# Modulation rows stored from adjacent partitions, tokens scaled in place, eight modulation pieces moved behind the recurrence

## The chip, the cores and the metric

The kernel runs on one core of a Trainium2 chip (trn2). The metric is the device time of one execution in microseconds (us); single instructions are given in nanoseconds (ns) where that is plainer. The engines are PE (matrix products, results in PSUM banks), DVE (vector operations), ACT (activations and copies), POOL (general vector work) and SP (issues most DMAs, in order). All engines run on their own and wait for one another by semaphores.

## The reference

Two layers of a diffusion trunk over 512 latent and 256 context tokens of width 1024, in float32. What matters here is the head of each layer:

```python
mod = sc @ w_ada[l] + b_ada[l]        # sc = silu(c), 6 x 1024 columns
modc = scc @ w_ada[l] + b_ada[l]      # scc = silu(c_ctx)
sh1, s1, g1, sh2, s2, g2 = jnp.split(mod[:, None, :], 6, axis=-1)
h = rmsnorm(x, norm1_g[l]) * (1 + s1) + sh1
p = jnp.split(h @ w_in[l], split_at, axis=-1)
```

The parts of `p` feed four mixers: A, a gated linear recurrence (HGRN); B, a long convolution (Hyena) whose filters are computed from small networks and turned into spectra; C, neighbourhood attention; D, latent attention. Their outputs go through one output projection, and a mixture of experts follows. The normalisation is `x * rsqrt(mean(x^2) + eps)` per token, then gain, scale and shift per column.

## The kernel before, in words

**Memory.** One large tile, the `arena`, holds nearly all working tiles as column ranges; `Scope` and `E.t` hand out the ranges, first fit. A second tile, `side`, holds weights in flight. PSUM banks come from small pools: `pw` has two banks and serves the projections (L1283), the modulation pieces (L1177, L1187) and, in layer 0, the transposes of the tokens.

**Order of the work.** The program is written in the order of the model, and the framework's scheduler places each engine's instructions: what stands earlier in the program goes first when it is ready, and later work fills the gaps. So what is written behind a loop can run beside it.

**Modulation (class `Ada`).** `w_ada` of a layer is used in 24 pieces. A piece (`step`) loads two halves of 512 KB by SP (L1175) into a ring buffer `araw`, does 8 products of 128x32 by 128x256 on PE (L1177; the profile records 16), four groups of input rows side by side in 32 PSUM partitions each, and ACT copies the result (L1182) into `part[g]`. After every eighth piece the four groups are added (L1187, a 0/1 matrix `sum4`), the bias is loaded (L1190, 128x512) and added on DVE (L1192), and two DMAs (L1194) store the row to DRAM (`modd`); the row's eight used lines lie 32 partitions apart (`row[v:128:32]`). `cols` (L1204 to L1210) turns the first row into columns, the scale `mcs` and the shift `mcb`, by four 128x128 transposes.

**Where the pieces run.** Pieces 0 to 7 of layer 0 run first (`boot`, 16 buffers). While they run, the first constants and the six token tiles `x` are loaded (L1461), at piece 4. The others are called by `more`: after each projection, `STEPS[n]` of them, and behind the recurrence, `STEPH` of them, through a ring of three buffers. Before, `STEPS` is one piece after each of the first eight projections, none after two and one after each of the last six, with `STEPH = 10`: 24 in all (16 of layer 0, 8 of layer 1).

**Head of a layer.** `row_scales` squares the token rows (ACT L1227, DVE L1224, a scratch `hfull`), forms `rsqrt` on DVE (L1132 to L1145) and scales an identity by it (L1232) for each of six token tiles. `normed_T` multiplies each 128x128 block of `x` by that scaled identity (L1247), which transposes and normalises at once; ACT (L1250) and DVE (L1251) apply scale and shift, and the high and low parts `hh`, `hl` are formed (L1252). Four latent and two context tiles, eight column blocks each: 48 blocks for a layer.

**Projections and filters in layer 0.** `Proj.cols` loads 128 columns of `w_in` (L1274), splits them (ACT L1258, POOL L1259) and does 24 matmuls for the latent and 24 for the context tokens (L1283). The order is two columns each for i, q, g, then four for z, the recurrence (`hgrn`, L219 to L313, six levels of DVE work L241 to L268 and then a serial scan L291), then six u for the convolution. Between the projections the filters are computed by the generator `spectra`: for each of three filters it loads `w3`, `decay`, `tun`, `fwd`, `rot`, folds the filter (`filter_fold`, L409 to L445, ends in the sum L443) and stores its spectra (`filter_spectra`, L460 to L469, stores `spd`). `FOLD0` and `FOLDS` say how many steps of it go where; all of it stands ahead of z.

## Time and profile before

| | |
|---|---|
| median of 3 runs | 2461.41 us (2459.84 to 2464.67) |
| profiled execution, its time | 2464.16 us |
| its span | 2462.1 us |
| PE busy | 2059.6 us (84%) |
| DVE busy | 1055.0 us (43%) |
| ACT, POOL busy | 614.7 us (25%), 586.8 us (24%) |
| HBM | 240 GB/s over the span |

Busy times are means over the whole span, in which layers 0 and 1 each go through a front (projections, mixers) and an expert stage that streams weights. The span is the profiled part of one execution; the time of that execution is the one with which its durations belong. Each L number is a line of the kernel.

### The profile page before, as it was taken

Reading aid. Unit: us, or ns where it says so; the run is one execution under the profiler, and the core shown is the slowest. Engines: PE = TensorE matmul, PEld = TensorE weight load, DVE = VectorE, ACT = ScalarE, POOL = GpSimd, SP = SyncE. Lnnn points to the kernel's source line nnn. Section 1 sums busy time; section 2 is a strip of 40 time slices with the busy share of each in tenths; the row PEclk is TensorE's granted clock in tenths of the full one; section 3 lists DMA queues with packets and bytes.
Section 4 is the critical chain, followed back from the end, with each engine's and each line's share of the span. In section 5 each row is a group of like instructions: output and inputs, shape, how many; then the busy total and the mean of one; then the engine's idle time right before and its main releaser. Section 6 shows DMA issues by size and latency. Waiting matters only on the chain.

```text
span 2462.1 us, 32352 instructions
## 1 busy us (share of the span) xinstructions
PE 2059.6 (84%) x11460; PEld 1200.1 (49%) x11460; DVE 1055.0 (43%) x2495; ACT 614.7 (25%) x1205; POOL 586.8 (24%) x477
## 2 busy tenths in 40 slices
PE   5888889999999588887777598899899688877775
PEld 2555667866679433322222286676668433222221
DVE  5753885546865622222112437754584611111111
ACT  2445632143541100000000235324352110000000
POOL 1553732312003211211111236331101212111111
PEclk7999999999999699999999799999999699999998
DMA  7343424301242799999999624431233799999996
GB/s 274 129 152 126 164 88 152 100 26 52 84 139 78 275 379 371 405 401 403 401 403 397 226 86 154 134 124 35 73 116 118 283 390 409 411 407 409 411 404 255
DMA packets 139316, 581.57 MB, mean 236 GB/s; under 512 B 23984, under 2 KB 47873, under 8 KB 88630
## 3 DMA queue, kind: packets, MB, share of 16 engines
q1 hardware_dynamic: 124054, 555.89, 58.4%
q0 software_dynamic: 15008, 22.36, 3.8%
q8 instruction: 151, 2.47, 0.4%
q14 instruction: 103, 0.84, 0.1%
HBM read 554.17 MB, written 36.80 MB: 240 GB/s over the span
## 4 chain that ended last, share of the span: by engine, by line
PE 32%; DMA 25%; another core or an unknown queue 18%; DVE 12%; issue 4%; ACT 3%; POOL 2%; SPq 0%; ACTq 0%; POOLq 0%; DVEq 0%
PE pw L1283 11%; DMA acc<-arena 8%; DMA out_dram<-arena 7%; DMA arena<-h2d,arena 6%; PE pw L1804 4%; PE pb L609 2%; PE pa L789 1%; PE pb L529 1%; PE pb L511 1%; DMA spd<-arena 1%; DVE arena L265 1%; DVE arena L266 1%; PE pb L592 1%; PE pb L995 1%
## 5 line engine op out<-in xcount | busy, mean ns | idle before, releaser
L995 PE MATMUL pb<-side,arena 128*64 128x512 f32 x1224 | 288.0, 604 | 45.7 <-DMA side<-in_w_moe 42.1
L999 DVE COPY arena<-pb 128x512 f32<-128x512 f32 x67 | 46.3, 691 | 502.9 <-PE pb L995 502.9
L995 PE MATMUL pb<-arena 128*64 128x512 f32 x920 | 221.1, 616 | 38.3 <-DMA arena<-in_w_moe 34.8
L1011 ACT ACTIVATE arena<-pb 128x256 f32<-128x256 f32 x67 | 25.8, 384 | 901.7 <-PE pb L1008 901.7
L1259 POOL TENSOR_TENSOR wl<-side,wh 128x1024 fp32r<-128x1024 f32 x52 | 125.6, 2416 | 399.3 <-ACT wh L1258 200.8
L995 PEld LDWEIGHTS pb<-side,arena 128*64 128x64 f32 x1224 | 81.1, 137 | 246.5 <-issue 126.8
L1283 PE MATMUL pw<-hh,wh 128*128 128x512 f32 (+1 forms) x720 | 170.1, 369 | 5.8 <-ACT arena L1559 2.1
L1026 DVE SCALAR_TENSOR_TENSOR arena<-pb,arena 128x512 f32<-128x512 f32 x67 | 50.3, 751 | 261.5 <-PE pb L1022 253.5
L1283 PE MATMUL pw<-hh,wl 128*128 128x512 f32 (+1 forms) x720 | 161.0, 357 | 0.0
L1283 PE MATMUL pw<-hl,wh 128*128 128x512 f32 (+1 forms) x720 | 158.2, 354 | 0.0
L995 PEld LDWEIGHTS pb<-arena 128*64 128x64 f32 x920 | 63.3, 140 | 189.9 <-issue 101.6
L1022 PE MATMUL pb<-side,arena 128*64 128x512 f32 x576 | 135.4, 609 | 22.4 <-DVE arena L1012 21.9
L1035 POOL DMA_INDIRECT acc<-arena x35 | 55.2, 1578 | 388.4 <-DVE arena L1030 341.6
L1283 PEld LDWEIGHTS pw<-hh,wh 128*128 128x128 f32 x720 | 119.5, 192 | 41.0 <-issue 15.0
L1022 PE MATMUL pb<-arena 128*64 128x512 f32 x496 | 115.7, 607 | 21.8 <-DVE arena L1012 20.2
L1283 PEld LDWEIGHTS pw<-hl,wh 128*128 128x128 f32 x720 | 117.2, 189 | 24.0 <-issue 8.2
L1283 PEld LDWEIGHTS pw<-hh,wl 128*128 128x128 f32 x720 | 117.3, 190 | 23.0 <-issue 8.0
L1035 POOL DMA_INDIRECT out_dram<-arena x32 | 50.9, 1590 | 311.8 <-DVE arena L1026 297.3
L973 POOL DMA_INDIRECT arena<-h2d,arena x67 | 69.8, 1042 | 187.4 <-issue 81.3
L1808 POOL TENSOR_TENSOR arena<-arena 128x256 f32<-128x256 f32 x40 | 30.3, 759 | 292.5 <-DVE arena L1807 277.4
L234 PE MATMUL pa<-arena 128*128 128x128 f32 x560 | 75.9, 283 | 18.7 <-DVE arena L241 4.7
L1008 PE MATMUL pb<-ident,arena 128*128 128x128 f32 x268 | 42.2, 280 | 56.3 <-DVE arena L999 54.5
(369 smaller groups left out, 3602.5 us busy)
## 6 DMA issues: line engine op xcount, KB each, us to landing
side<-in_w_moe SPq DMA_DIRECT2D x215, 1024.0 KB
arena<-in_w_moe SPq DMA_DIRECT2D x169, 1024.0 KB
side<-in_w_in SPq DMA_DIRECT2D x52, 512.0 KB
side<-in_w_ada SPq DMA_DIRECT2D x48, 512.0 KB
arena<-in_w_ada SPq DMA_DIRECT2D x48, 512.0 KB
arena<-in_w_out SPq DMA_DIRECT2D x16, 512.0 KB
arena<-in_x SPq DMA_DIRECT2D x12, 512.0 KB
spd<-arena SPq DMA_DIRECT2D x23, 256.0 KB
```

Source lines behind the costliest of these rows:

```text
L234: nc.tensor.matmul(ps[:, c], kx[:, c], q[:, c], start=True, stop=True)
L609: nc.tensor.matmul(po[64 * s:64 * s + 64], v[:, h * 64:h * 64 + 64], PT[s][:, j], start=(j == 0), stop=(j == len(V) - 1), skip_group_check ...
L973: E.gathered = nc.gpsimd.indirect_dma_start(out=xg, out_offset=None, in_=h2d, in_offset=bass.IndirectOffsetOnAxis(ap=gi, axis=0), **(dict( ...
L995: nc.tensor.matmul(pg[64 * s:64 * s + 64], xT[:, j // 4, j % 4, :], W[j // 2][:, (j % 2) * 1024 + s * 512:(j % 2) * 1024 + s * 512 + 512], ...
L999: nc.vector.tensor_copy(gu, pg)
L1008: nc.tensor.transpose(pt[:, c * 128:(c + 1) * 128], gu[:, c * 128:(c + 1) * 128], E.c["ident"])
L1022: nc.tensor.matmul(pd[64 * s:64 * s + 64], hT[:, c, :], W[4 + c // 2][:, (c % 2) * 1024 + s * 512:(c % 2) * 1024 + s * 512 + 512], start=( ...
L1026: nc.vector.scalar_tensor_tensor(y, pd, w[0], g2[0], op0=ALU.mult, op1=ALU.mult)
L1035: E.nc.gpsimd.indirect_dma_start(out=acc, out_offset=bass.IndirectOffsetOnAxis(ap=si, axis=0), in_=y, in_offset=None, compute_op=ALU.add, ...
L1259: (nc.vector if k % 2 else nc.gpsimd).tensor_sub(lo, src, hi.bitcast(F32))
L1283: nc.tensor.matmul(ps[:, :n], w[:, j, :], h[:, j, a:a + n], start=(i == 0), stop=(i == 23))
L1804: nc.tensor.matmul(ps[:, :256], o_[:, k, tt], w[:, k, :], start=(i == 0), stop=(i == 23))
```

## The change

- The sum of a modulation row goes into 8 adjacent partitions instead of 128: one accumulation over four groups with a new 0/1 constant `sum8`. The bias is loaded as 8x512, into the tile that then holds the row; the stores read four adjacent partitions each. `cols` transposes 8x128 blocks.
- `scale_rows` takes the place of `row_scales`: it multiplies the token tiles themselves by the row scale, in place, even ones on DVE and odd ones on ACT. `normed_T` transposes the blocks with the plain identity.
- `STEPS` has none in the first ten places, and `STEPH` is 18: the eight pieces that ran after projections 1 to 8 now come behind the recurrence, ahead of the u projections.
- The inputs of the first filter's spectra (2.06 MB) are loaded at piece 4 of `boot`, right after the tokens, into memory of their own; `rot` is loaded ahead of `fwd`.

```diff
@@ -1182,17 +1182,15 @@
         nc.scalar.copy(self.part[g][:, q * 256:(q + 1) * 256], ps[:, :256])
         if c % 8 == 7:
             m = c // 8
-            ps = E.pw()
+            ps = E.pw()[:8]
             for g in range(4):
-                nc.tensor.matmul(ps[32 * g:32 * g + 32], E.c["sum4"], self.part[g], start=True, stop=True,
-                                 skip_group_check=True)
-            bt = self.keep.t("adb", 512, F32, 1, P)
-            nc.sync.dma_start(bt, self.b[m])
-            row = self.keep.t("adp", 512, F32, 4, P)
-            nc.vector.tensor_add(row, ps, bt)
+                nc.tensor.matmul(ps, E.c["sum8"][:, g], self.part[g], start=(g == 0), stop=(g == 3))
+            row = self.keep.t("adr", 512, F32, 1, 8)
+            nc.sync.dma_start(row, self.b[m])
+            nc.vector.tensor_add(row, ps, row)
             for v in range(2):
                 nc.sync.dma_start(self.modd[v:v + 1, m * 2048:(m + 1) * 2048].rearrange("v (g c) -> (v g) c", g=4),
-                                  row[v:128:32])
+                                  row[4 * v:4 * v + 4])
             self.row = row
         return True
@@ -1201,21 +1199,20 @@
         E, nc = self.E, self.E.nc
         ps = E.pw()
         for q in range(4):
-            nc.tensor.transpose(ps[:, q * 128:(q + 1) * 128], self.row[:, q * 128:(q + 1) * 128], E.c["ident"])
-        v = ps.rearrange("p (q g m) -> p g q m", q=4, g=4)
+            nc.tensor.transpose(ps[:, q * 8:(q + 1) * 8], self.row[:, q * 128:(q + 1) * 128], E.c["ident"][:8, :8])
+        v = ps[:, :32].rearrange("p (q m g) -> p g q m", q=4, m=2)
         ob, os_ = (o.rearrange("p (g q) v -> p g q v", g=2) for o in (out_b, out_s))
         gn = gain.rearrange("p (g q) -> p g q", g=2)
         for g in range(2):
-            nc.vector.tensor_copy(ob[:, g], v[:, g, :, 0:2])
-            nc.vector.scalar_tensor_tensor(os_[:, g], v[:, 2 + g, :, 0:2], 1.0, bcast(gn[:, g].unsqueeze(2), P, 4, 2),
+            nc.vector.tensor_copy(ob[:, g], v[:, g])
+            nc.vector.scalar_tensor_tensor(os_[:, g], v[:, 2 + g], 1.0, bcast(gn[:, g].unsqueeze(2), P, 4, 2),
                                            op0=ALU.add, op1=ALU.mult)
-def row_scales(E, x, parts):
-
-
-    nc = E.nc
-    out = []
+def scale_rows(E, x, parts):
+
+
+    nc = E.nc
     for t0, nt in parts:
         rs = E.t("rs1", 4, bufs=2)[:, :nt]
         for i in range(nt):
@@ -1228,15 +1225,17 @@
         nc.vector.tensor_scalar(rs, rs, 1.0 / DM, EPS, op0=ALU.mult, op1=ALU.add)
         small_rsqrt(E, rs, "rs1", nt)
         for i in range(nt):
-            out.append(E.t("rs1d", P, bufs=6))
-            nc.vector.tensor_scalar(out[-1], E.c["ident"], rs[:, i:i + 1], None, op0=ALU.mult)
-    return out
+            xt = x[:, t0 + i]
+            if i % 2:
+                nc.scalar.mul(xt, xt, rs[:, i:i + 1])
+            else:
+                nc.vector.tensor_scalar(xt, xt, rs[:, i:i + 1], None, op0=ALU.mult)
 LATENT, CONTEXT = (0, 4), (4, 2)
-def normed_T(E, x, D, cs, cb, hh, hl, bank):
+def normed_T(E, x, cs, cb, hh, hl, bank):
     nc = E.nc
     for v, (t0, nt) in enumerate((LATENT, CONTEXT)):
@@ -1244,8 +1243,7 @@
         for j in range(8):
             ps = bank()[:, :nt * 128]
             for i in range(nt):
-                nc.tensor.matmul(ps[:, i * 128:(i + 1) * 128], x[:, t0 + i, j * 128:(j + 1) * 128], D[t0 + i],
-                                 start=True, stop=True)
+                nc.tensor.transpose(ps[:, i * 128:(i + 1) * 128], x[:, t0 + i, j * 128:(j + 1) * 128], E.c["ident"])
             h = E.t("hfull", 512, bufs=2)[:, :nt * 128]
             nc.scalar.activation(hh[:, j, cc], ps, AF.Identity, scale=cs[:, j, v:v + 1], bias=cb[:, j, v:v + 1])
             nc.vector.tensor_scalar(h, ps, cs[:, j, v:v + 1], cb[:, j, v:v + 1], op0=ALU.mult, op1=ALU.add)
@@ -1337,8 +1335,8 @@
 FLIGHT = 5
 LAG = 2
 AHEAD = 1
-STEPS = [1] * 8 + [0] * 2 + [1] * 6
-STEPH = 10
+STEPS = [0] * 10 + [1] * 6
+STEPH = 18
 BOOT = 4
 FOLD0 = 4
 FOLDS = [5] * 6
@@ -1441,6 +1439,10 @@
         tc.keep_in_program_order(nc.scalar.preload_act_table_set("natural_log_exp_and_others"))
+        def spectra_inputs(l, L):
+            return {k: E.load(f"f{k}", a) for k, a in (("w3", d[f"hy_w3{l}"]), ("decay", d[f"hy_decay{l}"]),
+                    ("tun", d[f"hy_tun_{L}"]), ("rot", d[f"hy_rot_{L}"]), ("fwd", d[f"hy_fwd_{L}"]))}
+
         sa = E.scope(high=True)
         adas = [Ada(E, csil, d[f"w_ada{l}"], d[f"b_ada{l}"], modd[l], sa) for l in range(2)]
         close_ring, _ = side(SIDE - 16384)
@@ -1459,8 +1461,10 @@
                 n1g = [E.const(f"n1g{l}", d[f"n1g{l}"]) for l in range(2)]
                 for t in range(6):
                     nc.sync.dma_start(x0[:, t], d["x"][t])
+                E.cur = fs
+                inputs = spectra_inputs(0, 512)
         sh = E.scope()
-        diag = row_scales(E, x0, (LATENT, CONTEXT))
+        scale_rows(E, x0, (LATENT, CONTEXT))
         adas[0].cols(n1g[0], mcs[0], mcb[0])
         boot.close()
         close_boot()
@@ -1469,8 +1473,7 @@
         def spectra():
             for l, L in ((0, 512), (1, 512), (0, 256)):
-                W = {k: E.load(f"f{k}", a) for k, a in (("w3", d[f"hy_w3{l}"]), ("decay", d[f"hy_decay{l}"]),
-                     ("tun", d[f"hy_tun_{L}"]), ("fwd", d[f"hy_fwd_{L}"]), ("rot", d[f"hy_rot_{L}"]))}
+                W = inputs if (l, L) == (0, 512) else spectra_inputs(l, L)
                 spd[l, L] = dr.tile([P, 2, L // 64 + 1, 256], F32, name=f"spd{l}{L}")
                 fold, nb = yield from filter_fold(E, L, rows[l, L], W)
                 yield
@@ -1519,9 +1522,9 @@
             if l:
                 E.cur = fs
                 sh = E.scope()
-                diag = row_scales(E, x0, (LATENT, CONTEXT))
+                scale_rows(E, x0, (LATENT, CONTEXT))
             E.cur = sh
-            normed_T(E, x0, diag, mcs[l], mcb[l], hh, hl, E.pf if l else E.pw)
+            normed_T(E, x0, mcs[l], mcb[l], hh, hl, E.pf if l else E.pw)
             sh.close()
             pr = Proj(E, hh, hl, d[f"w_in{l}"], hp, ring, between)
@@ -1843,7 +1846,7 @@
             if full:
                 sa = E.scope(high=True)
                 sa.reserve("adp", 512, 4)
-                sa.reserve("adb", 512, 1)
+                sa.reserve("adr", 512, 1)
                 adas[1].keep = sa
                 bring = E.scope()
                 bring.reserve("araw", 1024, max(1, 2 * B0))
@@ -1861,17 +1864,18 @@
-CONSTS = ("ident", "ones", "sum4", "ones64", "b16", "b32", "m96", "m32", "sel16", "sel32", "before", "miota", "mpc", "hmask")
+CONSTS = ("ident", "ones", "sum8", "ones64", "b16", "b32", "m96", "m32", "sel16", "sel32", "before", "miota", "mpc", "hmask")
 def constants():
     c = selectors()
     c.update(moe_consts())
     c["hmask"] = hgrn_masks()
-    s4 = np.zeros((128, 32), np.float32)
+    s8 = np.zeros((128, 4, 8), np.float32)
     for g in range(4):
-        s4[32 * g + np.arange(32), np.arange(32)] = 1
-    c["sum4"] = s4
+        for v in range(2):
+            s8[v::32, g, 4 * v + g] = 1
+    c["sum8"] = s8
     for L in (512, 256):
         c[f"hy_feats_{L}"] = hyena_feats(L)
         c[f"hy_tun_{L}"] = hyena_tunit(L)
@@ -1910,9 +1914,8 @@
         w = i["w_in"][l]
         d[f"w_in{l}"] = w[:, cols].reshape(8, 128, -1, 128).transpose(2, 1, 0, 3)
         d[f"w_ada{l}"] = i["w_ada"][l].reshape(2, 4, 128, 24, 256).transpose(3, 0, 2, 1, 4)
-        ba = np.zeros((3, 4, 32, 512), np.float32)
-        ba[:, :, :2] = i["b_ada"][l].reshape(3, 4, 1, 512)
-        d[f"b_ada{l}"] = ba.reshape(3, 128, 512)
+        ba = i["b_ada"][l].reshape(3, 4, 512)
+        d[f"b_ada{l}"] = np.concatenate([ba, ba], 1)
         d[f"n1g{l}"] = i["norm1_g"][l].reshape(8, 128).T
         d[f"n2g{l}"] = np.repeat(i["norm2_g"][l][None], 128, 0)
         d[f"n2c{l}"] = i["norm2_g"][l].reshape(8, 128).T
```

## Rows read from the trace of the kernel before

**Rows 1.** The page's part on the chain of waits, shares of the span by line
```profile
PE pw L1283 11%; DMA acc<-arena 8%; DMA out_dram<-arena 7%; DMA arena<-h2d,arena 6%; PE pw L1804 4%; PE pb L609 2%; PE pa L789 1%; PE pb L529 1%; PE pb L511 1%; DMA spd<-arena 1%; DVE arena L265 1%; DVE arena L266 1%; PE pb L592 1%; PE pb L995 1%
```

**Rows 2.** Stretches: length, busy us (instructions) of PE, weight loads, DVE, ACT, POOL; granted clock, DMA, GB/s
```profile
20.00:40.00 20.00, 12.96 (x81) 3.89 (x84) 9.31 (x22) 4.86 (x9) 0.00 (x0) 0.57 1.00 359
54.40:100.60 46.20, 37.36 (x194) 27.81 (x193) 38.81 (x56) 23.60 (x38) 24.43 (x17) 0.91 0.42 147
255.00:313.00 58.00, 49.92 (x442) 36.42 (x440) 57.01 (x76) 40.15 (x85) 46.41 (x47) 1.00 0.52 176
313.00:418.60 105.60, 92.63 (x738) 74.30 (x740) 72.00 (x161) 32.65 (x52) 24.01 (x17) 0.95 0.35 120
```

**Rows 3.** Order of events, layer 0's start: start us, us, engine, line, operation, [idle before]
```profile
23.39 5.87 SPq L1175 DMA_DIRECT2D side<-in_w_ada  x6
...
42.88 1.10 SPq L1194 DMA_DIRECT2D modd<-arena  x2
...
43.77 0.15 DVE L1210 SCALAR_TENSOR_TENSOR mcs<-pw,n1g 128x8 f32<-128x8 f32 x1
...
45.25 1.06 ACT L1227 ACTIVATE arena<-arena 128x1024 bf16<-128x1024 f32 x1 [4.28 <-DMA modd<-arena]
...
54.32 0.76 ACT L1250 ACTIVATE hh<-pw,mcb,mcs 128x512 fp32r<-128x512 f32 x1
```

**Rows 4.** Who waited for the tile modd, 0 to 600 us: us, times
```profile
  ACT arena L256: 4.9, 1
```

**Rows 5.** One line's instructions: count, min/median/max ns, first and last start, shapes
```profile
L1247 PE MATMUL pw<-arena x96: 273/275/582, 51.8 to 78.8; 128*128 128x128 f32 x96
...
L1204 PE MATMUL pw<-ident,arena x8: 272/273/329, 42.9 to 421.3; 128*128 128x128 f32 x8
...
L1232 DVE TENSOR_SCALAR arena<-ident,arena x12: 274/282/2328, 51.4 to 1407.1; 128x128 f32<-128x128 f32 x12
...
L377 DVE TENSOR_SCALAR arena<-arena x6: 277/407/418, 6.5 to 32.6; 64x512 f32<-64x512 f32 x4, 64x256 f32<-64x256 f32 x2
...
L1258 ACT CAST wh<-side x52: 1030/1047/1058, 53.2 to 1729.7; 128x1024 fp32r<-128x1024 f32 x52
```

**Rows 6.** The chain of waits, 79 to 235 us: start us, us, what
```profile
105.56 1.04 PE pw L1177 x16
...
112.86 2.49 DMA spd<-arena
...
184.10 4.57 DMA spd<-arena
...
221.99 3.38 DMA spd<-arena
...
227.65 3.39 DMA spd<-arena
```

**Rows 7.** Order of events on PE, single moments
```profile
233.93 1.08 PE L1177 MATMUL pw<-arena,csil 128*32 128x256 f32 x8 [3.28 <-ACT arena L1571]
...
236.52 1.39 PE L1187 MATMUL pw<-arena,sum 128*32 128x512 f32 x8
...
254.63 1.61 PE L234 MATMUL pa<-arena 128*128 128x128 f32 x13
...
380.57 2.88 PE L1283 MATMUL pw<-hh,wh 128*128 128x512 f32 x6 [0.64 <-DVE arena L478]
...
409.89 1.99 PE L1283 MATMUL pw<-hl,wh 128*128 128x512 f32 x8
```

**Rows 8.** Order of events in the recurrence: first and tenth piece, u, the row store
```profile
265.09 0.37 ACT L1182 COPY arena<-pw 128x256 f32<-128x256 f32 x1
...
312.56 0.37 ACT L1182 COPY arena<-pw 128x256 f32<-128x256 f32 x1
...
312.99 0.73 PE L1283 MATMUL pw<-hh,wh 128*128 128x512 f32 x2
...
330.79 0.50 SPq L1194 DMA_DIRECT2D modd<-arena  x1
```

## The prediction

> **What bounds the kernel now.** I read the chain of waits first, because the profile's busy shares are means over stages with different limits. Its shares by line [rows 1] put the projection matmuls (L1283) first at 11%, but three DMA groups of the expert stages hold as much again. The change touches none of those stages, and the expert weights start streaming only when the layer's front is done, so a gain in the front passes through to the end. That front, 0 to 420 us of layer 0, is what has to be read closely, then 1386 to 1425 us, where layer 1 starts.
>
> Next come the stretches [rows 2]. Between 54.4 and 100.6 us DVE is busy 38.8 of 46.2 us: the normalised transposes and the fold of the first filter are a DVE stage. From 313 to 418.6 us PE is busy 92.6 of 105.6 us: there the u projections fill everything the recurrence leaves, and PE is the bound. In between (255 to 313 us) DVE is busy 57.0 of 58.0: the six levels of the recurrence.
>
> Then the order of events at the start [rows 3]. The tokens are asked for just before the last six modulation loads (23.39 us). From 20 to 40 us the DMA moves 359 GB/s [rows 2]. The pieces asked for before the tokens are 5.2 MB and the tokens 3.1 MB, so at the rates of the first 40 us I estimate that the tokens have landed near 30 us. Yet ACT squares the first token row only at 45.25 us. The row names what it waited for: the store of the modulation row, issued at 42.88 us. That store reads its own row and the square writes scratch; there is no reason in the data. The list of who waited for that store has another such wait, 4.9 us at the first level of the recurrence [rows 4]. The store picks every 32nd partition of a tile; I take it that its footprint is judged as a block of the whole arena, so that anything later that writes the arena waits for it.
>
> **The change, part by part.**
>
> *Row stored from adjacent partitions; spectra inputs asked for early.* With the block gone, squares, scales and row scaling happen between 30 and 42 us, on DVE and ACT, which have room there (DVE busy 9.3, ACT 4.9 of 20 us [rows 2]). What then gates the first evacuation is the modulation column, ready at 43.92 us [rows 3], not the row scales: today ACT evacuates the first transposes at 54.32 us. But the spectra inputs (2.06 MB) now stand ahead of the last six pieces on SP's queue. At 359 GB/s they cost 5.7 us if all go first, nothing if all go behind. I take three quarters less the 0.24 MB that the small bias load saves: +3.6 us, because w3 (0.5 MB) is allocated first and so falls where the filter rows' tables lay, and must wait for them; it alone goes last. The column comes at 47.5 us, the first evacuation at 47.7: 6.6 us earlier.
>
> *Plain transposes.* A product with a scaled identity leaves two matmul records per block (96 for the 48 blocks of layer 0), a transpose one (8 for 8 blocks); each record is about 275 ns [rows 5]. PE's share of the 48 blocks of a layer halves. PE is not the bound there, though; it waits for DVE to free one of two banks. Of the 7.4 us in which DVE is idle between 54.4 and 100.6 us [rows 2] I take back 5, for PE comes back sooner and the small lower-bound work fits ahead of the column. Bounds are 0 and 7.4. The fold's end, today 100.6 us, so moves by 6.6 + 5 = **-12 us** (bounds -1 to -18).
>
> TensorE's granted clock was 0.57 of full speed from 20 to 40 us, mostly the lower of its two levels, 1.2 GHz, with PE busy 13 of 20 us; over the next stretch, with products with the scaled identity, it was 0.91 [rows 2]. By the Trainium skill (TensorE: Matmul & The Clock Gate, Part 4: PE-mode transpose) a transpose does not count as PE activity the way a matmul does, so 1.2 GHz would last through the new transposes; no run here shows it yet. By that the sum would be worse, see the third rival.
>
> *Eight modulation pieces moved from between the projections to behind the recurrence.* Each piece is two loads of 512 KB on SP, 16 matmul records, and one ACT copy; one row sum with its DVE add and two stores moves with them. What they cost where they are: after the last filter's wait, PE does a piece and the row sum from 233.93 to 237.91 us before the last two projections [rows 7], 4.0 us on the path. One more piece, 1.0 us, lies on the chain at 105.6 us [rows 6]. The spectra stores on the chain take 2.49 us when the queue is free, but 4.57 us and twice 3.4 us just behind modulation loads [rows 6]: 2.1 + 0.9 + 0.9 = 3.9 us. Together 4.0 + 1.0 + 3.9, **-9 us**; bounds 4 (only the serial part) and 16 (also PE's other seven pieces at 1.0 us each, which I cost at nothing because the filter chain, not PE, runs last there).
>
> What they cost where they go: PE work of 8 x 1.04 us and a row sum of 1.4 us, 10 us, in a stage of 163.6 us in which PE is idle for 8.1 us to 313 and for 13.0 us after it [rows 2]. Today the ten pieces pace themselves at (312.56 - 265.09) / 9 = 5.3 us, held by three load buffers, and the first u projection starts 0.4 us after the tenth copy, at 312.99 [rows 8]: pieces and projections share two PSUM banks in program order. With eighteen, u starts 30 to 40 us later. It loses cover, but what it loses it did slowly between the levels; behind the levels the projections run at PE's pace. I fill 3 us of idle: **+7 us**; bounds 0 and +15. ACT's eight copies (0.37 us each [rows 8]) and the 8.4 MB of loads have room (ACT 40 of 58 us, DMA share 0.52 [rows 2]). Queued behind a moved row store on SP are later modulation loads and the u weights: the store waits for its DVE add, and DVE has no room before the levels are over; SP issues today's one such store at 330.79 us, 18 us after the tenth copy [rows 8]. Now two rows sit there instead of one.
>
> *Row scaling in layer 1.* There the chain goes through the row scales. Scaling one identity takes 0.28 us, at worst 2.33 us [rows 5], so some 1 us for the four latent tiles. Scaling a 128x1024 row is bounded by twice the 64x512 form on DVE (0.41, so 0.8 us) and by the ACT cast of that size, 1.05 us [rows 5]: two each in parallel for the latent rows, 2.1 us, so +1.1 us. I take **+1 us**, bounds -1 (PE's quicker blocks come through) and +4 (a DVE scaling is held up as in the 2.33 us case).
>
> The row sum as one accumulation, the smaller bias load in five later places and the narrower column transposes I cost at nothing: the first two are covered by the recurrence or the filter chain, and without that cover they are worth half a microsecond each. The new order of the rotation and transform tables costs nothing either; if it did not hide, the next late thing would be the first spectra matmul.
>
> **Sum.** -12 - 9 + 7 + 1 = -13 us against the profiled execution, which took 2464.16 us (its span is 2462.1). That execution is 2.75 us above the median shown, 2461.41, so I predict 2461.41 - 13 = 2448 us.
>
> **Rivals.**
>
> *The tail slides (slower).* All six u projections wait for eighteen pieces, and what follows keeps its present pace behind them: the stage then grows by 8 x 5.3 = 42 us instead of 7, which gives 2448 + 35 = 2483 us. The mechanism is that the two PSUM banks go to pieces and unfinished row sums in program order; it turns the sign once the slide exceeds the 20 us net gained elsewhere, about half of the 42. For it: u's start right behind the tenth copy, and the late row store [rows 8]. Against it: 21 us of PE idle time in that stage, and levels that keep DVE full to 313 us whatever PE does [rows 2]. Chance 0.12.
>
> *The filter chain keeps its place.* The loads ahead of the last pieces cost the full 5.7 us and the DVE stage gives nothing back: the first term is -1. Then -1 - 9 + 7 + 1 = -2, or 2459 us. For it: DVE is busy 84% of that stage. Against it: none of the 10 us from column to first evacuation [rows 3] is needed once the row scales are early. Chance 0.15.
>
> *The clock stays low.* The first projection then starts at half clock. Six of its matmuls took 2.88 us where PE had stood still before, eight 1.99 us where it had not [rows 7], so 0.23 us more for each; for the 24 latent matmuls of one projection that is +5 us, or 2453 us. For it: the clock of 0.57 ahead of that stage [rows 2]. Against it: the matmuls of the fold are mixed in. Chance 0.08. The section of the Trainium skill named above is the reason to consider it.
>
> *The change does not do what it says:* squares still wait for the store, which itself comes 3.6 us later. The first term becomes about +3, and the time 2463 us. Against it: a plain slice of adjacent partitions leaves nothing to misjudge. Chance 0.05.
>
> **How the numbers follow.** My sum has 0.60, and its own range, from its bounds taken together but not all at one end, is 2434 to 2461. The whole range takes in the second and fourth rival above and a somewhat better front below: 2431 to 2465; what is left out is the slide and a front as good as all upper bounds. A measurement of this kernel can tell about 0.2%, 5 us, from no change. Faster by more: nearly all of my case and the clock's, and part of the second, 0.74. Within: the rest of the second, the fourth and an edge of mine, 0.15. Slower: the slide and a bad fourth, 0.11.
>
> **What would show it.** Right: the first square near 30 us with no wait for the store; first evacuation near 48 us; first spectra wait near 89 us; the recurrence's first matmul near 233 instead of 254.6 us [rows 7]; u starting some 90 us after that, and the stage to the first long transform 7 us longer. Wrong: a first evacuation still past 54 us, a recurrence that begins after 245 us, or PE idle while SP stands at a row store during the levels.

## The result, and the profile after

The changed kernel takes 2498.75 us in the median of its runs (2494.73 to 2500.08) where the kernel before takes 2461.48 beside it: a ratio of 1.0147, 95% interval 1.013 to 1.0165. It is 37 us slower, where 13 us faster was forecast. The profiled execution took 2494.73 us (span 2492.7), 30.6 us more than that of before.

| profiled execution | before | after |
|---|---|---|
| its time, its span (us) | 2464.16, 2462.1 | 2494.73, 2492.7 |
| PE, DVE busy (us) | 2059.6, 1055.0 | 2068.9, 1059.7 |
| first evacuation, sum that ends the first fold (start, us) | 54.32, 100.64 | 54.24, 96.95 |
| last u evacuation of layer 0, of layer 1 | 416.64, 1617.44 | 433.96, 1650.20 |

The stretches of after, in the columns of [rows 2]; the second and fourth run between the events that bounded them there, the fifth from PE's return behind the last filter step to the recurrence:

```profile
20.00:40.00 20.00, 10.62 (x36) 3.81 (x37) 14.73 (x40) 9.10 (x15) 0.00 (x0) 0.57 0.78 285
54.24:96.95 42.71, 29.64 (x119) 19.89 (x120) 38.59 (x59) 22.25 (x37) 24.12 (x17) 0.80 0.40 132
255.00:313.00 58.00, 48.41 (x408) 34.54 (x406) 58.00 (x78) 38.32 (x82) 47.98 (x48) 1.00 0.45 155
313.00:434.70 121.70, 109.16 (x894) 79.75 (x890) 71.31 (x162) 35.55 (x61) 23.77 (x18) 0.94 0.54 182
226.00:253.20 27.20, 27.14 (x144) 23.72 (x145) 0.00 (x0) 11.71 (x24) 4.79 (x2) 0.92 0.15 49
```

**The start** (answers to [rows 3]): order of events, SP and ACT.

```profile
29.93 1.04 ACT L1224 ACTIVATE arena<-arena 128x1024 bf16<-128x1024 f32 x1
...
31.79 0.33 SPq L170 DMA_DIRECT2D arena<-in_hy_w  x1
...
34.06 3.90 SPq L1175 DMA_DIRECT2D side<-in_w_ada  x6
...
53.18 0.61 SPq L1192 DMA_DIRECT2D modd<-arena  x2
...
54.24 1.45 ACT L1248 ACTIVATE hh<-pw,mcb,mcs 128x512 fp32r<-128x512 f32 x2 [3.07 <-PE pw L1246]
```

And the DMA queue's own waits on SP, 20 to 34 us (line, what it waited for: us in total, times, longest):

```profile
SPq L170 <- DVE arena L410: 9.1, 1, 9.1
```

The squares run at 29.93 us and wait for no store: the barrier is gone. But the first spectra load, `w3`, stands 9.1 us on SP's queue until its memory is free, and the six modulation loads behind it go out at 34.06 us instead of 23.39. The row is stored at 53.18 us instead of 42.88, and the first evacuation is where it was; the fold's end gains 3.7 us of the 12 forecast.

**Ahead of the recurrence** (to [rows 7]): POOL's last filter step in before (first row); then, in after, the same step, ACT's evacuation of the first z projection, PE.

```profile
231.99 1.26 POOL L468 TENSOR_TENSOR arena<-arena 128x512 f32<-128x512 f32 x1 [1.71 <-DVE arena L467]
...
223.62 1.26 POOL L468 TENSOR_TENSOR arena<-arena 128x512 f32<-128x512 f32 x1 [1.49 <-DVE arena L467]
...
224.92 0.60 ACT L1573 ACTIVATE arena<-pw 128x512 f32<-128x512 f32 x1 [2.10 <-POOL arena L468]
...
226.06 3.78 PE L1281 MATMUL pw<-hh,wh 128*128 128x512 f32 x8 [17.44 <-ACT arena L1574]
...
253.21 1.05 PE L234 MATMUL pa<-arena 128*128 128x128 f32 x8
```

The filters end 8.4 us earlier than before (223.62 against 231.99), but PE then has stood still for 17.4 us, because the first z evacuation waits for the last filter step; three z projections are left, and the recurrence starts 1.4 us earlier only. (In before a z evacuation waits for this step, too, but it is the complement of the second projection, for 3.17 us at 233.28 us.)

**Behind the recurrence** (to [rows 8]): the eighteenth copy, u, the second row store, the last u evacuation of layer 0; the last row is that of before.

```profile
355.06 0.66 SPq L1192 DMA_DIRECT2D modd<-arena  x2
...
355.55 1.67 PE L1281 MATMUL pw<-hh,wh 128*128 128x512 f32 x6
...
359.37 0.37 ACT L1182 COPY arena<-pw 128x256 f32<-128x256 f32 x1
...
433.96 0.56 ACT L476 ACTIVATE arena<-pw,arena 128x256 f32<-128x256 f32 x1
...
416.64 0.56 ACT L476 ACTIVATE arena<-pw,arena 128x256 f32<-128x256 f32 x1
```

u starts 42.6 us later than in [rows 8], and its last evacuation comes 17.3 us later. Two more losses lie beyond the steps of the prediction. At the output projection one of the four modulation rows, which before were asked for together at 604 to 615 us (first row below), is asked for at 739, behind weights, and DVE waits for it; and in layer 1 PE waits for modulation loads and then runs a row sum slowly, at a granted clock of 0.66 (the lower level, 1.2 GHz, for most of 1593.7 to 1596.6 us):

```profile
604.08 11.30 SPq L1510 DMA_DIRECT2D arena<-modd  x4
...
738.95 0.41 SPq L1513 DMA_DIRECT2D arena<-modd  x1
...
751.04 0.76 DVE L1810 TENSOR_TENSOR arena<-pw,arena 128x256 f32<-128x256 f32 x2 [5.63 <-DMA arena<-modd]
...
1592.88 1.08 PE L1177 MATMUL pw<-arena,csil 128*32 128x256 f32 x8 [3.96 <-DMA arena<-in_w_ada]
1593.71 2.87 PE L1187 MATMUL pw<-arena,sum 128*8 128x512 f32 x4
```

Of the 30.6 us between the two profiled executions 17.3 stand at the last u evacuation of layer 0, 24.4 at the first evacuation of layer 1 and 32.8 at its last u evacuation.

### The profile page after: what moved, and what is told of

Read it like the earlier page. It is cut to its first block, busy times and chain, and to the rows that moved or that the text cites. A ratio compares the mean times of both kernels' runs of the same rounds, so it can differ in the third digit from the quotient of the medians.

```text
span 2492.7 us, 32131 instructions
## 1 busy us (share of the span) xinstructions
PE 2068.9 (83%) x11364; PEld 1192.9 (48%) x11364; DVE 1059.7 (43%) x2489; ACT 620.0 (25%) x1211; POOL 586.4 (24%) x477
## 5 line engine op out<-in xcount | busy, mean ns | idle before, releaser
L999 DVE COPY arena<-pb 128x512 f32<-128x512 f32 x67 | 46.3, 692 | 494.7 <-PE pb L995 494.7
L1281 PE MATMUL pw<-hh,wh 128*128 128x512 f32 (+1 forms) x720 | 177.0, 378 | 21.5 <-ACT arena L1574 17.4
L1281 PE MATMUL pw<-hl,wh 128*128 128x512 f32 (+1 forms) x720 | 164.8, 363 | 0.0
L1035 POOL DMA_INDIRECT acc<-arena x35 | 55.2, 1578 | 385.3 <-DVE arena L1030 346.9
L234 PEld LDWEIGHTS pa<-arena 128*128 128x128 f32 x560 | 67.4, 193 | 45.5 <-POOL arena L265 20.0
```

Source lines behind the costliest of these rows:

```text
L234: nc.tensor.matmul(ps[:, c], kx[:, c], q[:, c], start=True, stop=True)
L999: nc.vector.tensor_copy(gu, pg)
L1035: E.nc.gpsimd.indirect_dma_start(out=acc, out_offset=bass.IndirectOffsetOnAxis(ap=si, axis=0), in_=y, in_offset=None, compute_op=ALU.add, ...
L1281: nc.tensor.matmul(ps[:, :n], w[:, j, :], h[:, j, a:a + n], start=(i == 0), stop=(i == 23))
```

## The experiments

All times are medians; each ratio is to the kernel before on the same chip (its medians there lie between 2462.66 and 2466.02 us), with its 95% interval. The events are starts in us, from the one profiled execution of each kernel.

| run | row store | first evac. | last filter step | last z evac. | last u evac. | layer 1: first, last u evac. | time | ratio |
|---|---|---|---|---|---|---|---|---|
| before | 42.88 | 54.32 | 231.99 | 254.87 | 416.64 | 1399.5, 1617.4 | 2461.48 | |
| after | 53.18 | 54.24 | 223.62 | 253.44 | 433.96 | 1423.9, 1650.2 | 2498.75 | 1.0147 |
| e1_steps_back | 54.30 | 55.36 | 232.23 | 267.58 | 431.88 | 1420.5, 1645.8 | 2493.85 | 1.0123 [1.0092, 1.0154] |
| e2_inputs_late | 50.02 | 51.30 | 222.09 | 251.49 | 434.96 | 1426.5, 1651.1 | 2494.73 | 1.0128 [1.01, 1.0157] |
| e3_row_only | 44.80 | 46.36 | 223.91 | 249.31 | 411.80 | 1395.9, 1618.7 | 2465.35 | 1.0014 [0.9997, 1.003] |
| e4_move_only | 41.90 | 53.94 | 229.96 | 250.97 | 419.92 | 1395.7, 1616.7 | 2471.31 | 1.0035 [1.0022, 1.0048] |
| e5_no_early_inputs | 51.73 | 52.80 | 227.36 | 248.16 | 424.79 | 1403.4, 1629.2 | 2476.41 | 1.0056 [1.0038, 1.0073] |
| e6_scale_only | 43.72 | 55.34 | 229.50 | 252.46 | 415.07 | 1394.3, 1608.1 | 2457.19 | 0.9974 [0.9962, 0.9986] |
| e7_inputs_only | 50.95 | 62.27 | 237.32 | 271.35 | 434.51 | 1418.0, 1639.0 | 2490.67 | 1.0111 [1.0083, 1.0138] |
| e8_row_own_bias | 44.66 | 46.17 | 223.63 | 250.60 | 412.73 | 1394.2, 1612.2 | 2465.96 | 1.0012 [0.9994, 1.0029] |
| g1_pairs_scale | 49.95 | 51.05 | 227.76 | 251.85 | 412.92 | 1390.5, 1604.8 | 2451.92 | 0.9944 [0.9925, 0.9964] |
| g2_pairs_scale_pad | 50.51 | 51.63 | 228.12 | 263.80 | 426.33 | 1407.2, 1623.5 | 2467.88 | 1.0014 [1.0, 1.0028] |
| g3_inputs_late_only | 42.61 | 53.80 | 232.28 | 265.70 | 428.66 | 1412.3, 1631.8 | 2483.55 | 1.0082 [1.0055, 1.0109] |
| g4_after_pad | 55.25 | 56.31 | 227.24 | 259.06 | 440.77 | 1425.7, 1649.0 | 2494.63 | 1.0115 [1.0089, 1.0141] |
| h1_g1_move | 49.70 | 50.80 | 226.23 | 247.05 | 422.39 | 1399.3, 1613.6 | 2461.12 | 0.9995 [0.9983, 1.0007] |
| h2_after_place | 55.13 | 56.19 | 230.73 | 253.51 | 429.42 | 1413.1, 1639.1 | 2480.23 | 1.0062 [1.004, 1.0083] |
| h3_g1_inputs_place | 49.95 | 51.07 | 228.57 | 250.56 | 412.57 | 1393.1, 1606.9 | 2454.75 | 0.9961 [0.9945, 0.9977] |
| h4_g1_one_sum | 51.97 | 52.97 | 227.42 | 253.01 | 416.46 | 1400.9, 1621.7 | 2468.63 | 1.0021 [1.0006, 1.0035] |
| i1_pairs_scale_layer1 | 43.80 | 45.36 | 222.94 | 244.65 | 407.21 | 1383.6, 1595.7 | 2445.05 | 0.993 [0.9908, 0.9952] |
| i2_pairs_only | 43.98 | 45.54 | 225.18 | 249.19 | 410.16 | 1389.4, 1602.5 | 2449.87 | 0.994 [0.9919, 0.996] |

### Four parts, undone or alone

My first theory was the rival of the slide: eighteen pieces ahead of u, and the rest is front.

```diff
# e1_steps_back, on the kernel after
-STEPS = [0] * 10 + [1] * 6
-STEPH = 18
+STEPS = [1] * 8 + [0] * 2 + [1] * 6
+STEPH = 10
```

> The changed kernel with the eight modulation pieces and their row sum put back between the first projections; all else as changed. Theory 1 (the move alone makes the tail of the recurrence longer: u starts at 355 instead of 313 us and its last evacuation comes at 434 instead of 416.6 us): the six u projections start some 58 us after the recurrence's first matmul again, PE no longer stands still for 17.4 us at 226 us, and the run is 16 to 24 us shorter than the changed kernel, 2475 to 2483 us. Rival 2 (the loss sits in the front or in the layer-1 start, where rows are scaled and transposed): the run stays within 5 us of the changed kernel, 2494 to 2504 us. Rival 3 (the loads ahead of the last six pieces cost as much as the barrier gave): says nothing of the tail, but the first evacuation stays at 54 us here.

Only 5 us came back. The stretch from the last z to the last u evacuation did fall, from 180.5 to 164.3 us, but the first z evacuation still waits (PE idle 12.36 us), and the recurrence starts 14 us later than in the changed kernel. Theory 1 is not the main cause.

```diff
# e2_inputs_late, on the kernel after
-                E.cur = fs
-                inputs = spectra_inputs(0, 512)
+        E.cur = fs
+        inputs = spectra_inputs(0, 512)
         sh = E.scope()
```

> The changed kernel with the five spectra inputs asked for behind the eighth modulation piece instead of with the tokens; all else as changed. Theory 3 (the first of those loads waits from 23 to 31.8 us for the memory of the filter rows, and the last six modulation loads stand behind it on SP's queue, so that the modulation row comes at 53.2 us): the row comes at 43 us or before, the first evacuation at 43.5 to 46 us instead of 54.2, the first fold ends some 8 to 10 us earlier, and the whole run is 5 to 10 us shorter than the changed kernel, 2489 to 2494 us. Rival (the last pieces are late because of DMA traffic, not because of the queue): the first evacuation stays at 51 us or later. By theory 1 the recurrence's tail stays as long as in the changed kernel (first matmul to last u evacuation about 181 us).

The row came 3 us earlier, not 10, and the evacuation at 51.30 us, which is in the rival's bracket: the queue is the smaller delay of the row, and another one was left, which was not the rival's DMA traffic (settled by the last two runs). The whole kernel gained 4 us, which is not clear of the two intervals.

```diff
# e3_row_only, on the kernel before; L1185 to L1194 and cols as in the change
...
-            row = self.keep.t("adp", 512, F32, 4, P)
-            nc.vector.tensor_add(row, ps, bt)
+            row = self.keep.t("adr", 512, F32, 1, 8)
+            nc.sync.dma_start(row, self.b[m])
+            nc.vector.tensor_add(row, ps, row)
...
-                                  row[v:128:32])
+                                  row[4 * v:4 * v + 4])
```

> The kernel before with the row stored from adjacent partitions alone (row sum as one accumulation, small bias load into the row's tile, narrow column transposes); the scaled identity, the old place of the spectra inputs and of the modulation pieces stay. If the strided store is what held the first squares: they run at 30 us without waiting, the first evacuation comes at 44 to 45 us instead of 54.3, and the run takes 2449 to 2456 us if the rest follows. Rival (later waits take the gain back: the filter chain is held elsewhere, or layer 1 pays for the bias load that now waits for the row's stores): the first evacuation moves as said, but the run is 2457 to 2470 us; the second row sum of layer 1 then ends some 7 us late against what surrounds it.

The barrier is the strided store: squares at 30.13 us, evacuation 8 us earlier, the filters' end too. Yet the time is that of before, as its rival had it: 3 of the 8 us are gone by the last u of layer 0, and in layer 1 a lead of 3.6 us at the first evacuation has become 1.2 us of delay at the last u.

```diff
# e4_move_only, on the kernel before
-STEPS = [1] * 8 + [0] * 2 + [1] * 6
-STEPH = 10
+STEPS = [0] * 10 + [1] * 6
+STEPH = 18
```

> The kernel before with the eight pieces and their row sum moved behind the recurrence, all else as before. Theory 1: filters end some 4 to 9 us earlier, but three z projections are left after them, so the recurrence starts within 3 us of the kernel before (254.6 us); u starts at 350 to 358 us, the last u evacuation comes 15 to 20 us later, and the run takes 2476 to 2485 us. Rival (the move pays as forecast, the loss is elsewhere in the change): 2452 to 2463 us.

7 us slower than the kernel before on its chip (2464.19): less than theory 1, more than its rival. Row (1.2 us) and move (7.1) alone add up to less than a quarter of the 37 us.

### The other parts, and the bias

```diff
# e5_no_early_inputs, on the kernel after
-                E.cur = fs
-                inputs = spectra_inputs(0, 512)
...
-                W = inputs if (l, L) == (0, 512) else spectra_inputs(l, L)
+                W = spectra_inputs(l, L)
```

> The changed kernel with the first filter's five spectra inputs loaded where they were before (by the filter itself, when the tokens' place is free again); row store, in-place scaling and the moved pieces stay. Theory 4 (the early loads are the main loss: they take memory above the tokens, so that the last filter's working rows come to lie at the bottom of the arena, where the z projections' outputs are put next, and the first z evacuation waits for the last filter step): the first z evacuation no longer waits for that step, PE's 17.4 us of idle time at 226 us falls below 9, the recurrence starts 8 us or more earlier than in the changed kernel (245 us or before), and the run takes 2464 to 2478 us. Rival 5 (the in-place scaling and the transposes are the main loss, since the runs with the row store or the move alone lost only 1 and 7 us): it stays at 2488 us or more.

22 us came back: theory 4. The first z evacuation runs at 199.54 us without a wait, PE's idle time is 7.27 us; the recurrence gained 5 us, not 8. Yet this kernel is still 14 us slower than the kernel before on its chip (2462.66).

```profile
199.54 0.60 ACT L1571 ACTIVATE arena<-pw 128x512 f32<-128x512 f32 x1
```

```diff
# e6_scale_only, on the kernel before; scale_rows as in the change, in both layers
-        diag = row_scales(E, x0, (LATENT, CONTEXT))
+        scale_rows(E, x0, (LATENT, CONTEXT))
...
-                nc.tensor.matmul(ps[:, i * 128:(i + 1) * 128], x[:, t0 + i, j * 128:(j + 1) * 128], D[t0 + i],
-                                 start=True, stop=True)
+                nc.tensor.transpose(ps[:, i * 128:(i + 1) * 128], x[:, t0 + i, j * 128:(j + 1) * 128], E.c["ident"])
```

> The kernel before with the token rows scaled in place and transposed plainly, nothing else. Theory 4: within 5 us of the kernel before, 2458 to 2469 us; the strided store still holds the squares to 45 us, the first evacuation stays at 52 to 55 us. Rival 5: 2480 us or more, with the extra time in the stage of the z projections or in the first 25 us of layer 1. The granted clock of the first projections tells whether plain transposes leave it low.

Rival 5 falls: scaling in place is a small gain, 5.5 us, a little more than theory 4's bracket allows.

```diff
# e7_inputs_only, on the kernel before; spectra_inputs and its use by the first filter as in the change
                     nc.sync.dma_start(x0[:, t], d["x"][t])
+                E.cur = fs
+                inputs = spectra_inputs(0, 512)
```

> The kernel before with the first filter's five spectra inputs asked for with the tokens, nothing else. Theory 4: the z projections' first evacuation waits for the last filter step, the recurrence starts 8 us or more later than in the kernel before, and the run takes 2476 to 2492 us. Rival 5: the loads only move within a queue that has room, 2455 to 2468 us.

Alone, early inputs cost 28 us: 8 at the first evacuation, 11 more between the last filter step (+5.3) and the last z evacuation (+16.5), and later a modulation row loaded at 735 us. The recurrence starts late as theory 4 has it.

```diff
# e8_row_own_bias, on e3_row_only
-            row = self.keep.t("adr", 512, F32, 1, 8)
-            nc.sync.dma_start(row, self.b[m])
-            nc.vector.tensor_add(row, ps, row)
+            bt = self.keep.t("adr", 512, F32, 1, 8)
+            nc.sync.dma_start(bt, self.b[m])
+            row = self.keep.t("adp", 512, F32, 4, P)[:8]
+            nc.vector.tensor_add(row, ps, bt)
```

> The kernel before with the row stored from adjacent partitions, as in the run of the row store alone, but the sum goes to a tile of its own, so that the next bias load no longer waits for the stores of the row before. Theory 6 (that wait is what made the run of the row store alone lose 9.3 us in layer 1 between 1600 and 1660 us): layer 1's last u evacuation comes with what surrounds it, and the run takes 2452 to 2459 us. Rival (the accumulation of the row sum is what costs there: it holds its bank until all four groups are in): the loss of 9 us stays, 2461 to 2468 us.

In the trace the last u of layer 1 is 6 us earlier than in e3, but the time did not change and lies in the rival's bracket: the bias is not what costs.

### Place in memory, and the sum

```diff
# g1_pairs_scale, on the kernel before, with the edit of e6
-            for v in range(2):
-                nc.sync.dma_start(self.modd[v:v + 1, m * 2048:(m + 1) * 2048].rearrange("v (g c) -> (v g) c", g=4),
-                                  row[v:128:32])
+            for g in range(4):
+                nc.sync.dma_start(self.modd[:, m * 2048 + g * 512:m * 2048 + (g + 1) * 512], row[32 * g:32 * g + 2])
```

> The kernel before with two edits: the modulation row keeps its 128 partitions and its four separate sums, but is stored as four pairs of adjacent partitions (four stores instead of two strided ones); the token rows are scaled in place and plainly transposed. Spectra inputs and modulation pieces stay. Theory 6b (in layer 1 the row store alone lost 9.3 us because the sum into one bank runs as a chain on PE, 3.5 us for a row, where the four separate sums run beside each other in 1.4 us): the first evacuation comes at 44 to 47 us, layer 1 loses nothing between 1600 and 1660 us, and the run takes 2444 to 2453 us. Rival (the loss in layer 1 has to do with the squares and stores no longer holding other work back, not with the sum): it is still there, and the run takes 2455 to 2462 us.

12 us faster than before. The layer-1 loss is gone with the separate sums; the first evacuation missed its bracket by 4 us (the last two runs show why).

```diff
# g2_pairs_scale_pad: g1_pairs_scale, inputs early as in e7 but placed as in e2; and
+            pad = Scope(E)
+            if full:
+                pad.reserve("pad", 4120, 1)
             F = [E.t("hF", NTOK, bufs=4) for _ in range(4)]
             K = [E.t("hK", NTOK, bufs=4) for _ in range(4)]
+            pad.close()
# g3_inputs_late_only: the kernel before, inputs early as in e7 but placed as in e2
# g4_after_pad: the kernel after with the pad of g2
```

> As the run with the four pair stores and in-place scaling, and the first filter's spectra inputs are asked for behind the eighth modulation piece, with the bottom 4120 columns of the arena kept free while the z projections' outputs are given their place, so that these do not fall on the last filter's working rows. Theory 4 (it is the place, not the early loads themselves): the first z evacuation does not wait for the last filter step, the recurrence starts no later than in the run without early inputs, and the time is within 6 us of that run, 2440 to 2455 us. Rival (early inputs cost something besides that place, as the layer's late load of the modulation row at 739 us): 2456 us or more.

> The kernel before with the first filter's spectra inputs asked for behind the eighth modulation piece, nothing else: their memory is taken while the tokens are still there, but no modulation load stands behind them. Theory 4 (place): the front is as before, the recurrence still starts 8 us or more late because the first z evacuation waits for the last filter step, and the modulation row of the output projection is still loaded late; 2472 to 2486 us. Rival (the queue: the load that waits for memory holds SP up): 2457 to 2466 us.

> The changed kernel, with the bottom 4120 columns of the arena kept free while the z projections' outputs are given their place; nothing else differs. Theory 4: the first z evacuation comes at its projection's end, near 218 us, without a wait for the last filter step, PE's idle time of 17.4 us at 226 us falls to 9 or less, the recurrence starts at 241 to 247 us instead of 253.2, and the run takes 2480 to 2492 us; below 2480 us if the longer tail of the recurrence comes from the place as well. Rival (place does not matter): 2494 to 2503 us.

g3 came as theory 4 has it: with the queue clear and the front as before, 20 us are lost. So the place costs more than the queue. The two pads missed, each in its rival's bracket. Their F rows lie free, but the complements K came onto other rows of the last filter. The wait of the first z evacuation in g3, and the next wait in g4:

```profile
233.57 0.60 ACT L1575 ACTIVATE arena<-pw 128x512 f32<-128x512 f32 x1 [0.91 <-POOL arena L468]
...
231.11 0.87 ACT L1578 ACTIVATE arena<-pw 128x512 f32<-128x512 f32 x2 [6.24 <-DMA spd<-arena]
```

In g4, that is, K waits for the store of the last spectra. That left the cause open, so the next runs put F and K in pairs.

```diff
# h2_after_place: the kernel after; h3_g1_inputs_place: g2 with this in place of its pad
+            pad = Scope(E)
+            if full:
+                pad.reserve("pad", 4120, 1)
+            F, K = [], []
+            for h in range(4):
+                F.append(E.t(f"hF{h}", NTOK, bufs=1))
+                K.append(E.t(f"hK{h}", NTOK, bufs=1))
+            pad.close()
```

> The changed kernel, with the z projections' outputs put in pairs (first, then its complement, then the second pair) above the bottom 4120 columns, so that the first pair lies where only the first filter weights of the last filter lay. The run that only kept the bottom free moved the wait from the first output to its complement, which then lay where the last spectra rows are stored from. Theory 4 (place): both evacuations of the first z projection come before 221 us without a wait for the last filter step or its store, the recurrence starts 6 to 10 us earlier than in the changed kernel, 243 to 248 us, and the run takes 2484 to 2493 us, as the longer tail stays. Rival (the z evacuations follow the filter because ACT is busy with it): the recurrence starts at 251 us or later, 2493 to 2503 us.

> The run with the four pair stores and in-place scaling, with the first filter's inputs asked for behind the eighth modulation piece and the z outputs put in pairs above the bottom 4120 columns. Theory 4: the 16 us that early inputs cost in the same setting with the bottom merely kept free fall away, and the run takes 2446 to 2457 us. Rival (early inputs cost elsewhere, too): 2458 us or more; then the table of delays shows where.

h3 lands within 3 us of g1, 13 us below g2: with the right place, inputs asked for behind the eighth piece cost nothing that these runs can tell. h2 gained 18.5 us from its place alone, but not where I said.

```profile
202.81 0.60 ACT L1579 ACTIVATE arena<-pw 128x512 f32<-128x512 f32 x1
...
233.30 0.87 ACT L1580 ACTIVATE arena<-pw 128x512 f32<-128x512 f32 x2 [7.29 <-DMA spd<-arena]
```

The first pair is out at 202.81 us; the second complement still waits for the spectra store until 233.30 us, and the recurrence starts as late as in the changed kernel. The gain came later: the last u is 4.5 us earlier, three of the four modulation rows at the output projection are asked for at 624 to 632 us again and DVE waits 0.2 us for them in all, and layer 1 starts 10.8 us earlier. Only places in the arena differ between the two kernels, so those waits, too, came from the place; what each of them costs was not separated.

```diff
# h4_g1_one_sum: g1_pairs_scale with sum, bias, stores and cols of e8_row_own_bias
# h1_g1_move: g1_pairs_scale with
-STEPS = [1] * 8 + [0] * 2 + [1] * 6
-STEPH = 10
+STEPS = [0] * 10 + [1] * 6
+STEPH = 18
```

> The run with the four pair stores and in-place scaling, but with the row sum as one accumulation onto eight partitions and two plain stores, the bias load in a tile of its own. Only the sum and its stores differ. Theory 6b: layer 1 loses 5 to 9 us between 1600 and 1660 us again, the recurrence's stretch in layer 0 some 2 to 4 us, and the run takes 2457 to 2464 us, against 2452 us with separate sums. Rival: within 3 us of 2452.

> The run with the four pair stores and in-place scaling, and the eight pieces with their row sum moved behind the recurrence. In the changed kernel without early inputs the stretch from the recurrence's first matmul to the last u evacuation grew by 19 us, in the kernel before with the move alone by 9. Theory 7 (the 10 us between are the row sums: as an accumulation into one bank each takes 3.5 us of PE in order, where four separate ones take 1.4, and holds one of two banks longer): here, with four separate sums, the stretch grows by 7 to 11 us against the run without the move, and the time is 3 to 10 us above that run's 2452 us. Rival (the stretch grows with the earlier start of the recurrence, since the tail ends when its loads allow): it grows by 16 us or more, 2464 us or more.

One sum in place of four costs 16.7 us, more than theory 6b said. On PE, 1550 to 1578 us, g1 (first two rows) and h4 (the next three); then the same four records of e3; last, the granted clock (the number behind the five busy times) of g1's first and h4's first row:

```profile
1552.55 1.06 PE L1187 MATMUL pw<-arena,sum 128*32 128x512 f32 x6
...
1556.03 1.47 PE L1187 MATMUL pw<-arena,sum 128*32 128x512 f32 x2 [0.49 <-ACT arena L1182]
```

```profile
1570.04 2.86 PE L1187 MATMUL pw<-arena,sum 128*8 128x512 f32 x4
...
1573.92 0.60 PE L1187 MATMUL pw<-arena,sum 128*8 128x512 f32 x1
...
1574.36 1.69 PE L1187 MATMUL pw<-arena,sum 128*8 128x512 f32 x3
```

```profile
1563.08 1.88 PE L1187 MATMUL pw<-arena,sum 128*8 128x512 f32 x4
```

```profile
1552.50:1553.65 1.15, 1.06 (x7) 0.15 (x6) 1.03 (x4) 0.00 (x1) 0.00 (x0) 1.00 0.88 291
1570.04:1572.90 2.86, 2.86 (x9) 0.63 (x5) 2.62 (x11) 0.00 (x0) 0.00 (x0) 0.66 0.46 135
```

Six records of separate sums, three groups, take 1.06 us at a granted clock of 1.00; four records into one bank take 2.86 at 0.66, behind a wait of 2.75 us for a modulation load, and the last four end at 1576.05. In e3, where the clock is 1.00 there, such four take 1.88, so about 1 us of the 2.86 is the clock; the chain is what is left, four records in 1.88 us against six in 1.06. The move alone costs 9.2 us in the setting of g1: the time is as theory 7 has it, but the stretch from the last z to the last u evacuation grew by 14.3 us (from 161.1 to 175.3), nearer to its rival.

```diff
# i2_pairs_only: g1_pairs_scale without the edit of e6
# i1_pairs_scale_layer1: g1_pairs_scale, layer 0 as before
-        scale_rows(E, x0, (LATENT, CONTEXT))
+        diag = row_scales(E, x0, (LATENT, CONTEXT))
         adas[0].cols(n1g[0], mcs[0], mcb[0])
```

> The run with the four pair stores and in-place scaling, but layer 0 keeps the scaled identity; only layer 1 scales its rows in place and transposes plainly. Theory 8 (in layer 0 ACT's squares and three row scalings of 1.06 to 1.15 us stand ahead of the modulation copies on ACT's queue, so that the row is stored at 49.95 us instead of 44.80 in the run of the row store alone): the row is stored at 43 to 46 us, the first evacuation comes at 44.5 to 47.5 us instead of 51.05, the first fold ends 2 us or more earlier, and the run takes 2443 to 2451 us against 2452. Rival (the row sum's accumulation, not the scaling, makes that difference, or plain transposes gain as much as the column loses): the store stays at 48 us or later, or the time is 2452 us or more.

> The kernel before with the four pair stores alone: the scaled identity stays in both layers. Theory 8 and 6b together: the barrier falls away as with the row store alone (squares at 30 us, store at 43 to 46 us, everything up to 225 us some 8 us earlier), and layer 1 loses nothing between 1600 and 1660 us, so 2450 to 2457 us; what the run with scaling in layer 1 is below this is what in-place scaling gives there, 0 to 6 us. Rival (what the row store gives in the front is taken back later whatever the sum): 2460 us or more.

Both as theory 8 says. ACT, 36 to 46 us, in g1 and in i1:

```profile
38.45 2.19 ACT L1231 ACTIVATE arena<-arena 128x1024 f32<-128x1024 f32 x2 [0.53 <-DVE arena L1145]
40.54 0.35 ACT L1182 COPY arena<-pw 128x256 f32<-128x256 f32 x1
43.36 1.15 ACT L1231 ACTIVATE arena<-arena 128x1024 f32<-128x1024 f32 x1 [2.46 <-DVE arena L1145]
44.41 0.35 ACT L1182 COPY arena<-pw 128x256 f32<-128x256 f32 x1
```

```profile
37.65 0.63 ACT L1182 COPY arena<-pw 128x256 f32<-128x256 f32 x2
40.77 0.37 ACT L1182 COPY arena<-pw 128x256 f32<-128x256 f32 x1 [2.49 <-PE pw L1177]
45.36 0.78 ACT L1275 ACTIVATE hh<-pw,mcb,mcs 128x512 fp32r<-128x512 f32 x1 [4.22 <-PE pw L1272]
```

In g1 ACT's row scalings stand ahead of the modulation copies, and the row comes 6 us later. PE shows it, too: at 40.95 us it has waited 4.84 us for such a copy.

```profile
40.95 1.08 PE L1177 MATMUL pw<-side,csil 128*32 128x256 f32 x8 [4.84 <-ACT arena L1182]
```

This is also the delay that e2 left: its row comes at 50.02 us, g1's at 49.95. i1 is the best kernel of the study, 0.7% below the kernel before; what scaling in layer 1 gives it over i2 (4.8 us) is within the intervals.

## Why the prediction was wrong

Single steps lead from the best setting with the scaling in both layers to the changed kernel: g1 2451.92, with the move (h1) 2461.12, with one sum instead of four, its bias and its stores (e5, which also has the new order of `rot` and `fwd`) 2476.41, with early inputs (after) 2498.75. That is +9.2, +15.3 and +22.3 us, against the 12 us that g1 gains on its kernel before: +34.8, and 37 were measured. These medians come from different chips; by the ratios the steps are +13, +15 and +22 us, against 14. Two of the prediction's own signs of being wrong came: a first evacuation past 54 us and a recurrence that begins after 245.

- **The barrier** was read rightly: a store that picks every 32nd partition holds later writers of the arena. With the four pair stores as the only edit (i2) the squares run at 30.23 us. Why such a store holds them is not shown.
- **First term, -12.** It measured -3.7 (100.64 to 96.95 us). The step that failed is that `w3` "alone goes last". SP's queue is in order, so a load that waits for its memory holds all six modulation loads. I also gave ACT room between 30 and 42 us by its busy share; what counted is who stands in front of its copies. With neither (i1), the first evacuation comes at 45.36 us and the filters end 9.1 us earlier, so most of the size was within reach. The lower bound of -1 is a slip of its own: 43.92 + 5.7 + 0.2 us with nothing from DVE gives a first evacuation at 49.8, which is -4.5.
- **Plain transposes, -5.** The stretch fell from 46.3 to 42.7 us, by 3.6, but not all of that is theirs. Without the early inputs it is 45.0 us (e5); with scaling and transposes as the only edit 44.5 (e6), so they give some 2 of the 5.
- **The clock** did stay lower: 0.80 against 0.91 in [rows 2], and 0.78 against 0.96 in g1 and i1, which differ in the scaling and the transposes of layer 0 alone (rows below). The first projection's first eight matmuls took 3.23 us, before 2.11, then 1.98 again: a price of about 1 us, not the 5 of that rival. By the Trainium skill (TensorE: Matmul & The Clock Gate, Part 4: PE-mode transpose) a transpose does not count as PE activity the way a matmul does; these rows agree with it.
- **Early inputs, priced at queue time only.** This is the largest term that failed: +3.6 us in the sum, 22 here (e5), 28 alone (e7). I had asked where the loads stand in the queue, not where their tiles lie. Allocated while the tokens are still there, they leave the bottom of the arena to the last filter's working rows, and the z outputs, which the same first fit puts there next, wait for them. Taking the loads off the queue's head gives back 4 us (e2, not clear of the intervals), another place for the z outputs 18.5 (h2), together the 22. But the wait of the z outputs is not the whole of it, since in h2 the recurrence starts no earlier. And this term alone did not turn the sign: without it (e5) the kernel is still 14 us slower.
- **Second term, -9.** With the move alone the last z evacuation comes 3.9 us earlier, 4.8 on g1: the lower bound. The pieces had filled PE time in which it waited for the filter chain anyway.
- **Third term, +7.** Alone, the stretch from there to the last u grew by 7.2 us, as forecast; on g1 by 14.3. In e4, h1 and e5 the last u came 3 to 8 us after that of the kernel before, though the recurrence started 4 to 8 us ahead of it, so what the move gains ahead of it is given back behind it. The two terms were to give -2; the move cost 7.1 us alone and 9.2 on g1. What binds that tail was not isolated.
- **One sum, "half a microsecond each".** I had put it at nothing, because the recurrence or the filter chain would cover it. Measured 15 to 17 us with its stores. Separate sums ran beside each other; one accumulation is a chain. How much of the 15 is PE time, how much the bank it holds, how much the waits for modulation loads and the lower clock behind them, and how much the stores was not separated.
- **Fourth term, +1** for layer 1: no run shows a cost; scaling there alone (i1 against i2) reads 4.8 us faster, within the intervals.
- **The rival that slides** gave 2483 us. Its 42 us came at the start of u (42.6), but 17 at its end, and 3 with the move alone (e4); the sign was right for another reason.

Rows for the clock: the stretches of g1 and i1 (the clock stands behind the five busy times), then the first projection on PE in after (two rows) and in before.

```profile
51.00:97.00 46.00, 35.55 (x142) 21.63 (x142) 40.56 (x60) 24.55 (x40) 24.93 (x17) 0.78 0.60 201
45.40:92.00 46.60, 36.04 (x193) 25.96 (x191) 41.77 (x61) 24.57 (x40) 26.04 (x18) 0.96 0.59 206
```

```profile
77.74 3.23 PE L1281 MATMUL pw<-hh,wh 128*128 128x512 f32 x8
80.81 1.98 PE L1281 MATMUL pw<-hl,wh 128*128 128x512 f32 x8
...
79.07 2.11 PE L1283 MATMUL pw<-hh,wh 128*128 128x512 f32 x8
```

## What to carry to other kernels

Before moving a load ahead, ask what it will wait for in an in-order queue, and what its tile's place pushes elsewhere: in a first-fit arena an allocation that comes earlier re-places all that follow, and costs where a late reader's rows are the next writer's. Where four small products already run side by side in four partition groups, keep them so and store the result in pieces of adjacent partitions; merging them into one accumulation cost 15 to 17 us here. Change one of five parts at a time: here two gains and three losses hid one another.

## What the runs showed of the hardware

Three row sums of 32 output partitions each, six records, took 1.06 us together (g1, at a granted clock of 1.00; in [rows 7] eight records took 1.39). I had read those rows without seeing that they overlap. In a chain into one bank four records took 1.88 us (e3, also at 1.00), one of them 0.59, so each further record 0.43; six would take 2.7 by estimate, 2.6 times as long as side by side. The Trainium skill (TensorE: Matmul & The Clock Gate, Part 3: Packing small matmuls — row/col tiling) says that products into different 32-partition strips run at once and states 2.38 times for three. This case is near that figure.

A modulation row asked for at 738.95 us, just behind expert weights and tokens, let DVE start at 751.04 only, 12 us later; for 5.63 us of them DVE had nothing else to do.
